# Holding the first store back until most of the fourth load has landed, and fewer, larger DMA packets at the start

## The chip, the cores and the metric

The kernel runs on one core of a Trainium2 chip. The metric is the device time of one execution, in microseconds. Before the change the median of 3 runs is 316.60 us (316.60 to 316.67).

## The reference

Each row of 1024 numbers is divided by the sum of its absolute values:

```python
batch, seq, dim = 32, 512, 1024          # x: float32, 64 MiB
sums = np.sum(np.abs(x), axis=-1, keepdims=True)
return (x / (sums + 1e-8)).astype(np.float32)
```

So 67.11 MB are read from HBM and 67.11 MB written, and every element is read once by a reduction and once by a multiplication in between.

## The kernel before

The input is seen as 16,384 rows of 1024 floats, 128 to each of the 128 partitions. They are cut into 11 tiles. Ten tiles have R = 12 rows per partition (49,152 bytes per partition, 6 MiB in all), the last, tile 10, has 8 (4 MiB). Tiles 0, 1 and 10 together make up a first block of 32 rows per partition that lies together in HBM; every other tile is a block of its own. `piece` gives the part of input or output that belongs to a tile.

There are BUFS = 4 tile buffers. A tile is loaded, normalized in its place and stored from there, so load i+4 can start only when store i has landed.

The order of work is written out by hand under `tc.manual_schedule()`; each engine runs its instructions in program order. Three engines matter:

- SP issues the loads (line 87), which run in DMA queue q1.
- ACT (ScalarE) issues the stores (line 97), which run in q10, and multiplies some rows of some tiles (line 68), one activation per row.
- DVE (VectorE) does the rest of a tile: the sum of absolute values over all its rows (line 47), the added constant (line 54), the reciprocal (line 56), one multiplication of `kv` rows with the reciprocals broadcast (line 58), and `kt` rows one by one (line 65). The table `split` has, for a tile, `kt` and the number `ks` of rows that go to ACT.

Both DMA queues run on the same 16 DMA engines. `max_dma_last_dim` sets how large a piece, in bytes, a DMA cuts the data of a partition into; a piece is a packet. WHOLE (49,152) makes one packet of a partition's 12 rows, HALF (24,576) two. Before the change loads 0 and 1 go in WHOLE packets, all others in HALF; store 0 is two DMAs, its first FIRST = 3 rows in packets of one row (4 * d = 4,096 bytes) and the other 9 in packets of 36,864. Store 8 is two halves, stores 9 and 10 go in WHOLE packets.

The loop over the tiles does compute, store and the load four tiles on. Store 0 is thus issued as soon as tile 0 is normalized, while loads 2 and 3 are still running.

Of the kernel before, what the change touches and what calls it, by code (L numbers as in the profile page):

```python
# [1 line left out]

# [4 lines left out]

FP32 = mybir.dt.float32
EPS = 1e-8


@with_exitstack
def kernel(
    ctx: ExitStack,
    tc: tile.TileContext,
    x: bass.AP,
    out: bass.AP,
):
    nc = tc.nc
    P = nc.NUM_PARTITIONS  # L20

    x_flat = x.flatten_outer_dims()
    out_flat = out.flatten_outer_dims()
    n, d = x_flat.shape

    R = 12
    BUFS = 4
    HEAD = 32
    per_partition = n // P
    assert n % P == 0 and (per_partition - HEAD) % R == 0  # L30
    rows = [R] * ((per_partition - HEAD) // R + 2) + [HEAD - 2 * R]

    def piece(flat, i):
        head = flat[: P * HEAD, :].rearrange("(p r) d -> p r d", p=P)
        if i < 2:
            return head[:, R * i : R * (i + 1), :]
        if i == len(rows) - 1:
            return head[:, 2 * R :, :]
        a = P * (HEAD + R * (i - 2))
        return flat[a : a + P * R, :].rearrange("(p r) d -> p r d", p=P)  # L40

    sbuf = ctx.enter_context(tc.tile_pool(name="sbuf", bufs=BUFS))
    stats = ctx.enter_context(tc.tile_pool(name="stats", bufs=len(rows)))

    def normalize(x_tile, k, kv, kt):
        s = stats.tile([P, R], FP32)
        nc.vector.tensor_reduce(  # L47
            out=s[:, :k],
            in_=x_tile[:, :k, :],
            axis=mybir.AxisListType.X,  # L50
            op=mybir.AluOpType.add,
            apply_absolute_value=True,
        )
        nc.vector.tensor_scalar_add(out=s[:, :k], in0=s[:, :k], scalar1=EPS)  # L54
        inv = stats.tile([P, R], FP32)
        nc.vector.reciprocal(out=inv[:, :k], in_=s[:, :k])  # L56
        if kv:
            nc.vector.tensor_mul(  # L58
                out=x_tile[:, :kv, :],
                in0=x_tile[:, :kv, :],  # L60
                in1=inv[:, :kv].unsqueeze(2).to_broadcast([P, kv, d]),
            )
        for r in range(kv, kv + kt):
            row = x_tile[:, r, :]
            nc.vector.tensor_scalar_mul(out=row, in0=row, scalar1=inv[:, r : r + 1])  # L65
        for r in range(kv + kt, k):
            row = x_tile[:, r, :]
            nc.scalar.activation(  # L68
                out=row,
                in_=row,  # L70
                func=mybir.ActivationFunctionType.Copy,
                scale=inv[:, r : r + 1],
            )

    last = len(rows) - 1
    split = {0: (3, 4), 1: (0, 3), 2: (0, 3), last - 1: (0, 2), last: (4, 4)}

    tiles = {}

    HALF, WHOLE = 24576, 49152
    FIRST = 3

    def load(i):
        x_tile = tiles[i] = sbuf.tile([P, R, d], FP32, name="x_tile")
        nc.sync.dma_start(out=x_tile[:, : rows[i], :], in_=piece(x_flat, i), max_dma_last_dim=WHOLE if i < 2 else HALF)  # L87

    def store(i):
        if i == 0:  # L90
            parts = [(0, FIRST, 4 * d), (FIRST, R, WHOLE)]
        elif i == last - 2:
            parts = [(0, R // 2, HALF), (R // 2, R, HALF)]
        else:
            parts = [(0, rows[i], WHOLE if i >= last - 1 else HALF)]
        for a, b, size in parts:
            nc.scalar.dma_start(
                out=piece(out_flat, i)[:, a:b, :],
                in_=tiles[i][:, a:b, :],
                max_dma_last_dim=size,  # L100
            )

    def compute(i):
        k = rows[i]
        kt, ks = split.get(i, (0, 0))
        normalize(tiles[i], k, k - kt - ks, kt)

    with tc.manual_schedule():
        for i in range(BUFS):
            load(i)  # L110
        for i in range(len(rows)):
            compute(i)
            store(i)
            if i + BUFS < len(rows):
                load(i + BUFS)


# [1 line left out]
_INS = ['x']  # L119
_OUTS = [((32, 512, 1024), 'float32')]  # L120


# [23 lines left out]
```

## Time and profile before

| what | us |
|---|---|
| median of 3 runs | 316.60 |
| the profiled execution | 316.77 |
| its span (first to last instruction) | 315.2 |
| VectorE busy | 260.6 |
| ScalarE busy | 18.5 |
| first load issued, tile 0's reduction starts | 0.73, 17.80 |
| first store issued (its two parts) | 36.78, 38.83 |
| second, third store issued | 61.95, 85.08 |
| load 4 issued | 76.83 |
| last store issued | 293.25 |

Sections of a profile row are read like this. A row of a window shows its bounds in us and its length, then for DVE, ACT and POOL the busy us with the number of instructions in brackets, the granted TensorE clock (TensorE isn't used here), the DMA share and GB/s. The DMA share is the mean busy share of the 16 DMA engines. In windows a packet is counted whole at its start, so that a short window can have a share above 1 or of 0. A row of the DMA queues shows the number of packets, MB and the share of 16 engines' span that they took. A row of waits shows who waited for what: total us, times, longest. In the packet counts, each DMA has besides its data 16 packets of 4 bytes, one from each DMA engine, that tell of its completion.

### The profile page before, as it was taken

The page shows a single profiled execution, that of the slowest core. Times are in us where ns is not written, and L with a number is a line of the kernel's source. Part 1 is how long each engine was busy: PE and PEld are TensorE (multiplying, and loading weights), DVE is VectorE, ACT ScalarE, POOL GpSimd, SP SyncE. Part 2 cuts the span into 40 slices and gives each one's busy share as a digit, 9 for nine tenths or more (in the row PEclk, how much of TensorE's full clock was granted, in tenths as well). Part 3 has the DMA queues.
Part 4 walks back from the last instruction along what each step waited for, and adds up shares of the span by engine and source line. Part 5 has one row for each costly group of instructions (what it writes and reads, how often), then busy time and mean ns, then how long its engine had stood idle before and what let it go on. Part 6 is the DMA issues. An engine that isn't in the chain of part 4 may idle for free.

```text
span 315.2 us, 172 instructions
## 1 busy us (share of the span) xinstructions
DVE 260.6 (83%) x50; ACT 18.5 (6%) x17; POOL 0.2 (0%) x4
## 2 busy tenths in 40 slices
DVE  0079999999999999989996997999699969999000
ACT  0010503004000000000000000000000000203200
POOL 0000000000000000000000000000000000000000
DMA  8999999999999999999999999999999999999997
GB/s 318 480 399 412 437 407 464 411 436 413 415 446 437 415 446 437 415 449 434 415 449 437 412 449 437 412 449 437 415 446 437 415 437 434 432 428 496 399 408 324
DMA packets 5761, 134.22 MB, mean 426 GB/s; under 512 B 385, under 2 KB 385, under 8 KB 769
## 3 DMA queue, kind: packets, MB, share of 16 engines
q1 hardware_dynamic: 2736, 67.11, 49.8%
q10 hardware_dynamic: 3024, 67.11, 49.4%
q14 instruction: 1, 0.00, 0.0%
HBM read 67.11 MB, written 67.11 MB: 426 GB/s over the span
## 4 chain that ended last, share of the span: by engine, by line
DVE 40%; DMA 33%; another core or an unknown queue 18%; ACT 1%; issue 0%; SPq 0%
DVE s L47 23%; DMA x_tile<-in_x_dram 17%; DMA out_dram<-x_tile 16%; DVE x_tile L58 15%; ACT x_tile L68 1%; DVE x_tile L65 1%; DVE inv L56 0%; DVE s L54 0%; SPq L87 0%
## 5 line engine op out<-in xcount | busy, mean ns | idle before, releaser
L47 DVE TENSOR_REDUCE s<-x_tile 128x12 f32<-128x12288 f32 (+1 forms) x11 | 138.2, 12562 | 29.8 <-DMA x_tile<-in_x_dram 29.8
L58 DVE TENSOR_TENSOR x_tile<-x_tile,inv 128x12288 f32<-128x12288 f32 (+3 forms) x10 | 113.6, 11358 | 0.5
L68 ACT ACTIVATE x_tile<-x_tile,inv 128x1024 f32<-128x1024 f32 x16 | 17.2, 1138 | 256.9 <-DVE inv L56 256.9
L65 DVE TENSOR_SCALAR x_tile<-x_tile,inv 128x1024 f32<-128x1024 f32 x7 | 4.8, 749 | 0.0
L56 DVE RECIPROCAL inv<-s 128x12 f32<-128x12 f32 (+1 forms) x11 | 2.5, 226 | 0.4
L68 ACT ACT_TABLE_LOAD x1 | 1.3, 1283 | 17.8 <-DMA x_tile<-in_x_dram 17.8
L54 DVE TENSOR_SCALAR s<-s 128x12 f32<-128x12 f32 (+1 forms) x11 | 1.9, 174 | 0.4
L130 POOL MEMSET const-bfloat16-1.0<- 128x1 bf16 x1 | 0.1, 101 | 0.0
L130 POOL MEMSET const-uint8-127<- 128x1 uint8 x1 | 0.1, 101 | 0.0
L130 POOL MEMSET const-float32-0.0<- 128x1 f32 x1 | 0.1, 98 | 0.2 <-issue 0.2
L130 POOL MEMSET const-float32-1.0<- 128x1 f32 x1 | 0.1, 98 | 0.0
## 6 DMA issues: line engine op xcount, KB each, us to landing
x_tile<-in_x_dram SPq DMA_DIRECT2D x10, 6144.0 KB, 36.9
out_dram<-x_tile ACTq DMA_DIRECT2D x8, 6144.0 KB, 49.1
out_dram<-x_tile ACTq DMA_DIRECT2D x2, 3072.0 KB, 33.4
out_dram<-x_tile ACTq DMA_DIRECT2D x1, 4608.0 KB, 37.9
x_tile<-in_x_dram SPq DMA_DIRECT2D x1, 4096.0 KB, 32.2
out_dram<-x_tile ACTq DMA_DIRECT2D x1, 4096.0 KB, 20.9
out_dram<-x_tile ACTq DMA_DIRECT2D x1, 1536.0 KB, 29.3
```

What stands on the lines that cost most here:

```text
L47: nc.vector.tensor_reduce(out=s[:, :k], in_=x_tile[:, :k, :], axis=mybir.AxisListType.X, op=mybir.AluOpType.add, apply_absolute_value=True,)
L54: nc.vector.tensor_scalar_add(out=s[:, :k], in0=s[:, :k], scalar1=EPS)
L56: nc.vector.reciprocal(out=inv[:, :k], in_=s[:, :k])
L58: nc.vector.tensor_mul(out=x_tile[:, :kv, :], in0=x_tile[:, :kv, :], in1=inv[:, :kv].unsqueeze(2).to_broadcast([P, kv, d]),)
L65: nc.vector.tensor_scalar_mul(out=row, in0=row, scalar1=inv[:, r : r + 1])
L68: nc.scalar.activation(out=row, in_=row, func=mybir.ActivationFunctionType.Copy, scale=inv[:, r : r + 1],)
L130: nc = _bacc.Bacc("TRN2", target_bir_lowering=False, num_devices=1)
```

## The change

The first store waits for a part of the fourth load. Load 3 becomes two DMAs: the first carries 10.5 of the tile's 12 rows of each partition (REST = 10,752 floats, 43,008 bytes), the second the last 1.5 (6,144 bytes). After the work on tiles 0 and 1, ACT gets a small activation that reads one element per partition of tile 3's first row, and so waits for the first of the two DMAs; store 0 stands behind it in ACT's program, and store 1 behind store 0. Tiles 0 and 1 are both computed ahead of it. Store 0 is one DMA in WHOLE packets instead of two DMAs. Loads 2 and 3 go in WHOLE packets too (load 3 in one packet per partition for each of its two parts). In tile 0 one row moves from VectorE's row operations to its broadcast multiplication.

```diff
-    split = {0: (3, 4), 1: (0, 3), 2: (0, 3), last - 1: (0, 2), last: (4, 4)}
+    split = {0: (2, 4), 1: (0, 3), 2: (0, 3), last - 1: (0, 2), last: (4, 4)}
...
-    FIRST = 3
+    REST = R * d - 3 * d // 2
 
     def load(i):
         x_tile = tiles[i] = sbuf.tile([P, R, d], FP32, name="x_tile")
-        nc.sync.dma_start(out=x_tile[:, : rows[i], :], in_=piece(x_flat, i), max_dma_last_dim=WHOLE if i < 2 else HALF)
+        size = WHOLE if i < BUFS else HALF
+        if i < BUFS - 1 or i >= BUFS:
+            nc.sync.dma_start(out=x_tile[:, : rows[i], :], in_=piece(x_flat, i), max_dma_last_dim=size)
+            return
+        flat = x_tile.rearrange("p r d -> p (r d)")
+        source = piece(x_flat, i).rearrange("p r d -> p (r d)")
+        for a, b in ((0, REST), (REST, R * d)):
+            nc.sync.dma_start(out=flat[:, a:b], in_=source[:, a:b], max_dma_last_dim=size)
 
     def store(i):
-        if i == 0:
-            parts = [(0, FIRST, 4 * d), (FIRST, R, WHOLE)]
-        elif i == last - 2:
-            parts = [(0, R // 2, HALF), (R // 2, R, HALF)]
-        else:
-            parts = [(0, rows[i], WHOLE if i >= last - 1 else HALF)]
-        for a, b, size in parts:
+        parts = [(0, R // 2), (R // 2, R)] if i == last - 2 else [(0, rows[i])]
+        for a, b in parts:
             nc.scalar.dma_start(
                 out=piece(out_flat, i)[:, a:b, :],
                 in_=tiles[i][:, a:b, :],
-                max_dma_last_dim=size,
+                max_dma_last_dim=WHOLE if i == 0 or i >= last - 1 else HALF,
             )
...
+    def wait_for_loads():
+        seen = stats.tile([P, 1], FP32, name="seen")
+        nc.scalar.activation(out=seen, in_=tiles[BUFS - 1][:, 0, :1], func=mybir.ActivationFunctionType.Copy)
+
     with tc.manual_schedule():
         for i in range(BUFS):
             load(i)
+        compute(0)
+        compute(1)
+        wait_for_loads()
         for i in range(len(rows)):
-            compute(i)
+            if i > 1:
+                compute(i)
             store(i)
             if i + BUFS < len(rows):
                 load(i + BUFS)
```

## The prediction

> **What bounds the kernel now.** I read the page first, then the stretches (busy time, DMA share and GB/s of a window), then waits and DMA issues.
>
> ```profile
> span 315.2 us, 172 instructions
> DVE 260.6 (83%) x50; ACT 18.5 (6%) x17; POOL 0.2 (0%) x4
> ...
> DMA  8999999999999999999999999999999999999997
> ...
> q1 hardware_dynamic: 2736, 67.11, 49.8%
> q10 hardware_dynamic: 3024, 67.11, 49.4%
> ...
> HBM read 67.11 MB, written 67.11 MB: 426 GB/s over the span
> ```
>
> The DMA engines are busy 99.2% of the span (49.8 + 49.4), q1 (SP) with loads, q10 (ACT) with stores. VectorE is busy 83% only. So the time is bytes over rate, plus start and end; the question is where the rate falls.
>
> ```profile
> 0.00:4.00 4.00, 0.00 (x0) 0.00 (x0) 0.20 (x4) 1.00 0.64 197
> 4.00:36.00 32.00, 18.10 (x4) 5.55 (x5) 0.00 (x0) 1.00 1.00 432
> ...
> 36.00:66.00 30.00, 29.90 (x9) 3.23 (x3) 0.00 (x0) 1.00 1.01 424
> ...
> 66.00:80.00 14.00, 13.90 (x4) 3.23 (x3) 0.00 (x0) 1.00 1.00 434
> 80.00:160.00 80.00, 78.14 (x13) 0.00 (x0) 0.00 (x0) 1.00 1.00 433
> 160.00:240.00 80.00, 71.74 (x13) 0.00 (x0) 0.00 (x0) 1.00 1.00 433
> ```
>
> The last number of a row is GB/s, the one before it the DMA share. Loads alone (4 to 36) run at 432, stores alone (66 to 80) at 434, both together (80 to 240) at 433. Mixing directions therefore costs nothing by itself. One stretch lies lower: 36 to 66, in which the first store's three-row part lies beside the rest of loads 2 and 3. One-microsecond windows show two costs in it:
>
> ```profile
> 13.00:14.00 1.00, 0.00 (x0) 0.00 (x0) 0.00 (x0) 1.00 1.81 786
> ...
> 33.00:34.00 1.00, 1.00 (x1) 1.00 (x2) 0.00 (x0) 1.00 0.91 393
> ...
> 61.00:62.00 1.00, 1.00 (x2) 0.00 (x0) 0.00 (x0) 1.00 1.07 459
> 62.00:63.00 1.00, 1.00 (x1) 0.00 (x0) 0.00 (x0) 1.00 1.51 459
> ```
>
> A packet is counted where it starts. 786 GB/s for 1 us is 16 packets of 49,152 bytes, one per DMA engine, 1.81 us each; 393 is 16 of 24,576, 0.91 us each; 459 is 16 of 24,576 and 16 of 4,096, so a small one takes 1.07 - 0.91 = 0.16 us. From 62 to 63 the same 32 packets took 1.51: 0.44 us lost on all engines. The trace's packet records give the finer figures used below: 159 ns for 4,096 bytes, 912 for 24,576, 1364 for 36,864, 1815 for 49,152, which is about 9 ns a packet plus 36.74 ns per 1000 bytes.
>
> ```profile
> DVE s L47 <- DMA x_tile<-in_x_dram: 29.8, 6, 17.8
> ...
> SPq L87 <- DMA out_dram<-x_tile: 242.1, 8, 63.3
> ```
>
> VectorE waits for loads, and SP's loads wait for stores (a buffer comes free): both hang on the DMA rate. DMA issues (last number: us from issue to landing) of load 0 and store 10:
>
> ```profile
> x_tile<-in_x_dram SPq DMA_DIRECT2D x1, 6144.0 KB, 17.0
> ...
> out_dram<-x_tile ACTq DMA_DIRECT2D x1, 4096.0 KB, 20.9
> ```
>
> **The change, part by part.** The sum is made against the profiled execution: 316.77 us, its span 315.2 and 1.6 around it, 0.17 above the median of 316.60.
>
> *Whole packets in store 0.* Before, each DMA engine carries 24 packets of 4,096 bytes and 8 of 36,864: 24 x 0.159 + 8 x 1.364 = 14.73 us. After, 8 of 49,152: 8 x 1.815 = 14.52. All of it is on the bound: **-0.21**.
>
> *Whole packets in loads 2 and 3.* Load 2: 16 x 0.912 = 14.59 becomes 14.52, **-0.07**. Load 3 becomes 8 packets of 43,008 and 8 of 6,144, by the line above 8 x 1.589 + 8 x 0.235 = 14.59: **0**. The extra load costs SP about 0.4 us of issue (its issues took 0.37 to 0.61 us) before 3 us, while load 0 transfers until 17.8.
>
> *A rule against this part.* Row first: the 4,096-byte pieces took 0.16 us, 25.8 GB/s an engine against 27.1 in a 49,152-byte packet. The Trainium skill (DMA: Bandwidth & Descriptors, Specifications) has line rate from 512 bytes up; read strictly, both packet edits would bring 0 instead of 0.28. I go by the row.
>
> *The slow loads of 36 to 66.* In the packet records the loads' packets between 36.9 and 64.3 took together 0.71 us per DMA engine above their usual 0.912 each: 0.13 until 56, 0.58 from 61 to 64.3 (0.44 of it is the row above). Bounds: all of it goes (-0.71), or none (0). I take **-0.71**: loads and stores of 24,576 bytes lie side by side from 80 to 279 and next to no packet is late there, so it isn't the mixture; small store pieces beside loads are what this stretch alone has, and after the change none are left, nor any load beside the first store's start.
>
> *The new wait.* Loads come first, 14.5 us each. The DMA rows put load 0's landing at 0.73 + 17.0 = 17.7; load 1's at about 32.3 and load 2's would be at 46.8. The 10.5 rows add 8 x 1.589 = 12.7: landing seen at L = 59.5. What is left then? The 1.5 rows are 8 x 0.235 = 1.88 us for each engine. The completion writes of load 0 lie between 16.85 and 17.44 in the records, and waiting engines went on at 17.80, so an engine has been 0.35 to 0.95 us into the rest at L: 0.93 to 1.53 remain, mean 1.24. What has to happen: ACT wakes (0.05, its table load began 17.85 against 17.80), does the 128x1 copy, issues the store (0.04), and the first packets start. The copy is not in the trace: at least 0.10 (the 128x1 memset on POOL), at most 1.13 (ACT's 128x1024 row); nearest is VectorE's 128x12 operation with 0.17, so I take 0.2. Issue to first packet: load 0 was issued at 0.73 on idle DMA engines and its packets start at 1.74 to 2.40, 1.16 later in the mean. Together 0.05 + 0.2 + 0.04 + 1.16 = 1.45, less 1.24: the DMA engines idle **+0.2**. Low end 0 (a copy of 0.1 and earliest start 1.0). High end: store 0 before was issued at 36.78 and its first packet started at 40.54, 3.75 later; then 0.29 + 3.75 - 1.24 = +2.8. I read that delay as queueing, some three load packets of 0.91 (2.7) taken ahead on each engine plus 1.0; load 4, issued at 76.83 behind 24,576-byte stores, started at 80.45, 3.6 later, which fits. Ahead of the new store stand only 0.235 us packets, already counted in the 1.24.
>
> *A second rule.* The row says 1.0 to 1.67 from issue to first packet. The Trainium skill (DMA: Bandwidth & Descriptors, Latency and other measured facts) has about 0.6 us for a DMA issued from SP or ACT; by it the need is 0.89 and the gap 0, which makes the sum 0.2 lower.
>
> *First packets of a stream.* The first 16 packets of load 0 took 0.70 us longer in the mean than 1.815 (hence 197 GB/s in the first 4 us). If the first store's do the same on an idle machine, +0.7; the first store packets before took 159 ns like all others, so I take **0** and keep 0.7 as the end.
>
> *What is queued behind the wait.* On ACT: store 0, store 1 and tile 2's three rows (ready at 75). VectorE does not wait: tile 0 has six broadcast rows (5.49 x 6/5 = 6.6) and two row operations (1.5) instead of 5.49 + 2.0, so it ends 0.5 later, and tile 1 at 62.4. Store 1 is then queued while store 0 transfers until about 75.5, so q10 doesn't run dry. The moved row costs 0: store 0 isn't issued before 59.8 anyway. SP's load 4 waits for store 0, landing at about 75.9 against 38.83 + 37.9 = 76.7 before: no later than now, and while store 1 keeps the engines full.
>
> *The end.* Store 10, issued at 293.25, lands 20.9 later though its 4 MB need 9.7: more than 10 us in the queue. VectorE could be 10 us later and cost nothing; if that cover went, the end would follow VectorE one to one.
>
> Sum: -0.21 - 0.07 - 0.71 + 0.2 = -0.79. 316.77 - 0.79 = 315.98 in the profiled form, **315.8** as median.
>
> **Rivals.**
> 1. *The slow loads stay*, elsewhere: the stall at 62 came once, on all engines, and I have no row that ties it to a store packet. For it: the small packets from 46 to 61 went along without it. Then -0.08: 316.5, no measurable change.
> 2. *The first store starts slowly* like load 0: +0.7, giving 316.5. For it: the 197 GB/s row. Against it: write packets never show lateness here.
> 3. *The other side: the hand-over leaves the DMA engines idle.* Everything depends on 1.24 us of cover. If issue to first packet is 3.75 as for store 0 before, not 1.16, the gap is 2.8 and the time 315.8 + 2.6 = 318.4. It decides (above 317.23) when the gap passes 1.6, which is 2.6 us from issue to first packet. Against it: the queueing reading fits two starts.
> 4. *Nothing changes* because the loads pace everything: excluded for the 0.28 of packets, since the engines are full either way.
>
> **How the numbers follow.** Forecast 0.48, own range 315.4 to 316.3; rival 1 0.22; rival 2 0.14; rival 3 0.12 (a smaller delay gives 317.2 to 318.4); others 0.04. The runs agree within 0.02%, so 0.2% (0.63 us: below 315.97, above 317.23) is about what a measurement can tell from no change. Faster: 0.36 of the forecast, 0.02 of rival 1: 0.38. Slower: 0.12 of rival 3, 0.03 of rival 2 with a wider gap, 0.02 others: 0.17. Same: 0.45. The range reaches from 315.4 (all gains, no gap) to 317.5 (no gains from the slow loads, plus 0.7 and some more gap), leaving out some 0.03 below and 0.13 above.
>
> **What would show it.** In the profile after: no packets below 8 KB but completions and 128 of 6,144; first store issued at about 59.8; windows of 1 us without 1.51 at 459; a window from 61 to 75 at 434; between 60 and 62 at most 0.3 us without packets. Wrong if that hole is 1 us or more, if late packets return around 60, or if load 4 lands after VectorE is done with tile 3 (111.8).

## The result, and the profile after

The change made the kernel slower: 317.63 us median (317.04 to 318.17, 8 runs) against 316.61 (316.46 to 316.68, 8 runs), a ratio of 1.0032 with a 95% interval of 1.002 to 1.0044. The runs of the changed kernel fall into two groups, four from 317.04 to 317.27 and four from 318.00 to 318.17; those of the kernel before lie within 0.22 us. The profiled execution took 317.27 us, 0.50 more than that of the kernel before, with a span of 315.6 against 315.2.

The page of the changed kernel, its head and the DMA queues:

```profile
span 315.6 us, 170 instructions
DVE 260.9 (83%) x49; ACT 18.7 (6%) x18; POOL 0.2 (0%) x4
...
q10 hardware_dynamic: 2624, 67.11, 49.6%
q1 hardware_dynamic: 2624, 67.11, 49.6%
```

5248 data and completion packets instead of 5760: the packets did become fewer. The DMA engines are as busy as before (99.2%), so the time is still theirs. Its stretches, with the bounds that were used for the kernel before (last two numbers: DMA share and GB/s):

```profile
4.00:36.00 32.00, 18.18 (x4) 5.55 (x5) 0.00 (x0) 1.00 1.02 442
36.00:66.00 30.00, 29.90 (x8) 3.43 (x4) 0.00 (x0) 1.00 0.97 419
66.00:80.00 14.00, 13.90 (x4) 3.23 (x3) 0.00 (x0) 1.00 1.07 441
80.00:160.00 80.00, 77.70 (x13) 0.00 (x0) 0.00 (x0) 1.00 1.00 427
160.00:240.00 80.00, 71.80 (x10) 0.00 (x0) 0.00 (x0) 1.00 1.01 433
```

With packets of 49,152 bytes the GB/s of a window depend on how many packets happen to start in it, so GB/s is to be divided by the share: bytes for each microsecond that the engines call themselves busy. 4 to 36 gives 433 and 36 to 66 gives 432, where the kernel before had 420 (424 at a share of 1.01). The slow stretch from 36 to 66 is gone. But 66 to 80 gives 412, where it had 434, and 80 to 160 gives 427 at a full share. One-microsecond windows find the place:

```profile
78.00:79.00 1.00, 1.00 (x1) 0.78 (x1) 0.00 (x0) 1.00 1.12 467
79.00:80.00 1.00, 1.00 (x1) 0.00 (x0) 0.00 (x0) 1.00 1.58 442
80.00:81.00 1.00, 1.00 (x1) 0.00 (x0) 0.00 (x0) 1.00 0.55 123
81.00:82.00 1.00, 1.00 (x1) 0.00 (x0) 0.00 (x0) 1.00 0.88 369
82.00:83.00 1.00, 1.00 (x1) 0.00 (x0) 0.00 (x0) 1.00 0.97 418
```

442 GB/s in one microsecond are 18 packets of 24,576 bytes; at 0.912 us each they would make a share of 1.03, and the row shows 1.58. In the packet records, a store packet on each of the 16 DMA engines that started between 79.66 and 80.20 took 1.46 to 1.81 us, up to twice its time. All engines lose 0.8 us there, and then the first packets of load 4 start, at 81.29. In the same place the kernel before lost nothing:

```profile
79.00:80.00 1.00, 1.00 (x1) 0.00 (x0) 0.00 (x0) 1.00 0.97 418
80.00:81.00 1.00, 1.00 (x1) 0.00 (x0) 0.00 (x0) 1.00 0.97 418
81.00:82.00 1.00, 1.00 (x1) 0.00 (x0) 0.00 (x0) 1.00 0.91 393
```

There load 4 began at 80.45 beside the same store 1, in the same packets. The waits of VectorE hardly moved, 30.2 us for loads in all (29.8 before).

**The ledger.** I call *late time* the sum, over packets, of what they took beyond their usual duration (9 ns and 36.74 ns per 1000 bytes), divided by 16 engines. From 6 us on it is 0.71 us before and 1.20 after. The usual durations of all packets sum to 0.27 us less. The completions of the last store come at 313.28 to 313.83 before and at 313.52 to 314.32 after: the engines end 0.35 later in the mean, and they end 0.24 us further apart, which makes the last one 0.49 later. So -0.27 from packets, +0.44 late time (with the start, where it fell by 0.05), +0.18 that the records don't assign (short gaps between packets), +0.14 from the spread of the ends: +0.49, and the span grew by 0.47. This is the ledger of an execution of the faster group; what makes the other four about 0.9 us longer is not in it.

### The profile page after: what moved, and what is told of

It reads as the page before. It is cut to its first block, busy times and chain, and to the rows that moved or that the text cites. A ratio compares the mean times of both kernels' runs of the same rounds, so it can differ in the third digit from the quotient of the medians.

```text
span 315.6 us, 170 instructions
## 1 busy us (share of the span) xinstructions
DVE 260.9 (83%) x49; ACT 18.7 (6%) x18; POOL 0.2 (0%) x4
## 2 busy tenths in 40 slices
DMA packets 5248, 134.22 MB, mean 425 GB/s; under 512 B 384, under 2 KB 384, under 8 KB 512
## 4 chain that ended last, share of the span: by engine, by line
DVE 38%; DMA 33%; another core or an unknown queue 18%; issue 3%; ACT 1%; SPq 0%; DVEq 0%
DVE s L47 23%; DMA x_tile<-in_x_dram 17%; DMA out_dram<-x_tile 15%; DVE x_tile L58 13%; DVE x_tile L65 1%; ACT x_tile L68 1%; DVE inv L56 0%; DVE s L54 0%; SPq L89 0%; DVEq L151 0%; DVEq L58 0%
## 5 line engine op out<-in xcount | busy, mean ns | idle before, releaser
L47 DVE TENSOR_REDUCE s<-x_tile 128x12 f32<-128x12288 f32 (+1 forms) x11 | 138.2, 12562 | 30.2 <-DMA x_tile<-in_x_dram 30.2
```

What stands on the lines that cost most here:

```text
L47: nc.vector.tensor_reduce(out=s[:, :k], in_=x_tile[:, :k, :], axis=mybir.AxisListType.X, op=mybir.AluOpType.add, apply_absolute_value=True,)
```

## The experiments

Each kernel is an edit of the kernel before or of the changed kernel. Late times are those of the one profiled execution of each kernel, whose time and span stand in the table; it can lie away from the median, by 1.1 us with whole packets at 80 and by 0.8 with half tiles. Letters in the expectations name theories: A, the wait brings the stall; B, an accident; C, one stall in every execution, at the first meeting of large stores and loads; D, large first store packets bring the loss; E, I, the held store makes the meeting at 80 stall, whatever went before; F, G, the stall grows with the packets, or is a fixed latency; H, a pause of some 20 us without loads makes it; L, the first longer spell of loads beside stores costs it, and later ones are free.

| kernel | median, us | before in the same runs | profiled (its span) | late time 6 to 36 | 36 to 66 | 66 to 84 | 84 to 140 |
|---|---|---|---|---|---|---|---|
| before (profile) | | | 316.77 (315.2) | 0.00 | 0.69 | 0.01 | 0.00 |
| changed | 317.63 | 316.61 | 317.27 (315.6) | 0.01 | 0.07 | 0.94 | 0.18 |
| the same again | 317.32 | 316.56 | 318.02 (316.4) | 0.02 | 0.34 | 1.03 | 0.18 |
| packets only | 317.38 | 316.56 | 317.38 (315.4) | 0.00 | 1.29 | 0.00 | 0.00 |
| wait only | 317.59 | 316.56 | 317.61 (315.8) | 0.01 | 0.18 | 0.98 | 0.13 |
| wait for 12 rows | 318.65 | 316.56 | 318.63 (316.7) | 0.00 | 0.09 | 0.97 | 0.13 |
| FIRST = 4 | 316.76 | 316.60 | 316.74 (315.1) | 0.09 | 0.43 | 0.07 | 0.13 |
| early scratch store | 319.96 | 316.60 | 319.91 (318.1) | 0.63 | 0.08 | 0.97 | 0.13 |
| whole packets at 80 | 319.26 | 316.60 | 320.40 (318.8) | 0.00 | 0.04 | 1.57 | 0.87 |
| quarter packets at 80 | 317.87 | 316.60 | 317.40 (315.8) | 0.01 | 0.13 | 1.01 | 0.16 |
| load 4 late | 316.63 | 316.59 | 316.80 (315.2) | 0.00 | 0.61 | 0.01 | 0.01 |
| half tiles | 319.04 | 316.59 | 319.87 (317.9) | 0.01 | 0.20 | 1.41 | 0.39 |
| small loads in the pause | 318.14 | 316.59 | 317.79 (316.1) | 0.00 | 0.03 | 0.88 | 0.22 |
| 3 rows early, 4,096 bytes | 316.78 | 316.57 | 316.58 (315.0) | 0.01 | 0.62 | 0.02 | 0.01 |
| 1 row early, 4,096 bytes | 316.71 | 316.57 | 316.62 (315.0) | 0.01 | 0.02 | 0.69 | 0.11 |
| 3 rows early, 12,288 bytes | 317.16 | 316.57 | 317.28 (315.7) | 0.00 | 0.56 | 0.84 | 0.12 |
| loads 2 and 3 whole | 316.69 | 316.57 | 316.63 (315.0) | 0.01 | 0.68 | 0.01 | 0.00 |
| wait for 4 rows | 316.86 | 316.52 | 316.93 (315.3) | 0.01 | 1.09 | 0.00 | 0.00 |

### The changed kernel again

> The changed kernel again, unaltered, on another occasion. Its 8 runs fell into two groups, 317.0 to 317.3 and 318.0 to 318.2, and its trace shows one stall of all DMA engines of about 0.8 us at 79.7 to 82, when load 4's first packets come. Theory A (a stall that the wait brings, at the return from stores alone to loads beside stores): the stall is there again near 80, the time stays 0.5 to 1.5 us above the kernel before, and if the profiled run is of the slower group a second stall of some 0.9 us shows in it. Theory B (an accident of that one execution): no stall near 80, and a time of 315.8 to 316.3.

317.32 us (317.24 to 318.02), ratio 1.0028 (1.0016 to 1.004). The stall is there again, late time 1.00 from 77 to 84. B falls. The profiled execution was the longest of the six (318.02); it has no second stall of 0.9, which A expected. Between its span and that of the profiled execution above lie 0.78 us: 0.35 are late time, most of it in the loads before the first store (0.27 from 36 to 66), and 0.42 come because its last engine ends 0.89 us behind the mean of the 16, not 0.47. Why the engines end further apart in some executions stays open.

### Each half of the change alone

The kernel before with whole packets and no wait:

```diff
-max_dma_last_dim=WHOLE if i < 2 else HALF)
+max_dma_last_dim=WHOLE if i < BUFS else HALF)
...
-            parts = [(0, FIRST, 4 * d), (FIRST, R, WHOLE)]
+            parts = [(0, R, WHOLE)]
```

> The kernel before with whole packets alone: store 0 as one DMA of 49,152-byte packets, loads 2 and 3 in whole packets; no wait, load 3 in one DMA, the old split of tile 0. Theory A (the loss comes from the wait): 316.6 - 0.28 = 316.3 if the stall at 62 us stays somewhere, 315.6 to 315.8 if that stall came from 4,096-byte pieces. Theory C (a stall of 0.6 to 0.9 us comes once in every execution, the first time that large store packets lie beside loads): a stall at about 40 us, when store 0's first packets start beside load 2, and 316.3. Theory D (large first store packets bring the loss): 317 or more.

317.38, ratio 1.0025 (1.0015 to 1.0034): slower without any wait. Windows of this kernel, at the start of store 0 and at load 4's old place:

```profile
40.00:44.00 4.00, 4.00 (x1) 0.00 (x0) 0.00 (x0) 1.00 1.15 369
78.00:84.00 6.00, 6.00 (x1) 0.33 (x1) 0.00 (x0) 1.00 1.02 438
```

369 over 1.15 is 321 GB/s: the stall, 1.29 us of late time, is where store 0's whole packets first meet loads. From 78 to 84 nothing is late. The 317 of D and the stall at 40 of C both came, but the stall is larger than C's 0.6 to 0.9. Only part of the time is the stall's, though: the span grew by 0.27 us (0.59 more late time, 0.36 less in the usual durations of the packets), while the time outside the span was 1.9 to 2.0 us in all nine runs, where the kernel before has 1.6 to 1.7. What that part is, the profile doesn't show; four more kernels of the table have 1.7 to 2.0 there.

The wait alone, with the packets and the row split of before (in the changed kernel, store 0 again in two DMAs, loads 2 and 3 in half packets):

```diff
-        size = WHOLE if i < BUFS else HALF
+        size = WHOLE if i < 2 else HALF
...
-        parts = [(0, R // 2), (R // 2, R)] if i == last - 2 else [(0, rows[i])]
+        if i == 0:
+            parts = [(0, FIRST, 4 * d), (FIRST, R, WHOLE)]
...
```

> The changed kernel with the packets and the row split of the kernel before: the wait, with load 3 in two DMAs, is what is left of the change. Store 0 is two DMAs again, 3 rows in 4,096-byte packets and 9 rows; loads 2 and 3 in half packets. Theory A (the wait brings the stall): a stall near 80 us as in the changed kernel, and 317.3 + 0.28 = 317.6 to 318.5. Theory D (whole packets bring it): 316 to 316.5. Theory C: a stall too, near 80.

317.59 (1.0032; 1.0021 to 1.0044), 0.93 us late from 77 to 84: A and C as expected, and D falls as the only cause. Either half of the change alone brings a stall of its own, in different places. Together they make one.

### The price of the hand-over

```diff
-        if i < BUFS - 1 or i >= BUFS:
+        if True:
```

> The changed kernel with load 3 as one DMA, so that the first store waits for all 12 rows and no 1.5 rows are left to transfer beside the hand-over. This measures the cover. By the prediction's sum the DMA engines then idle 1.45 us and the skew of the completions, 1.5 to 2.0 us at 59 to 63, against next to none in the changed kernel, and the time is 1.3 to 1.9 us above it. A rival: the hand-over costs nothing since the end is bound elsewhere, and the time equals the changed kernel's.

318.65, 1.33 us above the changed kernel in the same runs (317.32). The windows of this kernel:

```profile
60.00:61.00 1.00, 1.00 (x1) 0.00 (x0) 0.00 (x0) 1.00 0.01 0
61.00:62.00 1.00, 1.00 (x1) 0.20 (x1) 0.00 (x0) 1.00 0.00 0
62.00:63.00 1.00, 1.00 (x2) 0.00 (x0) 0.00 (x0) 1.00 1.89 786
```

Its last load packets end at 60.66 in the mean and the first store packets start at 62.22: 1.56 us of idle engines, inside the expected 1.5 to 2.0. (The ends are those of the completion writes.) In the changed kernel the two lie 0.02 us apart. The 1.5 rows do what the prediction's sum said, and the loss isn't there.

### Where large stores first meet loads

FIRST = 4 in the kernel before, so that the small packets outlast load 3:

```diff
-    FIRST = 3
+    FIRST = 4
```

> The kernel before with FIRST = 4 instead of 3: store 0's part in 4,096-byte packets has four rows, so that it outlasts load 3 and the large packets of store 0's second part never lie beside loads; large stores first meet loads near 80 us, as in the changed kernel. In every trace so far one stall of all DMA engines comes where large store packets first lie beside loads: 62 us before (0.5 us), 40 us with whole packets alone (1.2), 79 to 82 us with the wait (0.85 to 0.95). Theory C (one such stall in every execution, at the first meeting of large stores and loads): no stall at 62, one of 0.8 to 0.9 us near 80, and 316.6 - 0.5 + 0.85 + 0.07 = 317.0. Theory E (the meeting at 80 is harmless in a kernel without the wait, as it is in the kernel before, and only the wait makes it stall): no stall at all and 316.6 - 0.5 + 0.07 = 316.2.

316.76, ratio 1.0006 (0.9997 to 1.0015): no measurable change. The stall at 62 is gone, and from 78 to 84, where large stores now first meet loads, next to nothing is late (0.07 us). So C, as worded, falls. But E's 316.2 didn't come either:

```profile
38.00:42.00 4.00, 4.00 (x3) 0.00 (x0) 0.00 (x0) 1.00 1.01 397
78.00:84.00 6.00, 6.00 (x1) 0.46 (x1) 0.00 (x0) 1.00 0.92 393
```

397 GB/s lie at a share of 1.01 where 0.92 would do: the late loads moved to the start of the small stores, 0.35 us of late time in these four. All late time of this kernel is 0.72 us, as in the kernel before (0.71).

A short early store, in the changed kernel:

```diff
+    scratch = nc.dram_tensor("scratch", (32, 6, d), FP32, kind="Internal").ap()
+    def early_store():
+        nc.scalar.dma_start(out=scratch, in_=tiles[0][:32, :6, :], max_dma_last_dim=HALF)
...
+        early_store()
         compute(0)
```

> The changed kernel with one more store, of 32 packets of 24,576 bytes (two for each DMA engine) from the first 6 rows of tile 0 as loaded, into a scratch tensor in HBM, issued when load 0 has landed at 17.7 us, beside load 1. Its bytes cost 0.79 MB / 433 GB/s = 1.8 us. Theory C (one stall in an execution, at the first meeting): a stall of 0.9 to 1.8 us near 20 us and none near 80; the time is 317.3 + 1.8 + 0 to 0.9. Theory E (it is this meeting, after 20 us of stores alone): the stall near 80 stays as it is, 0.85 us, and 317.3 + 1.8 = 319.1 with no stall near 20, or about 320 with one more.

319.96. Two stalls: 0.63 us near 20, and 0.97 near 82. Two store packets on each engine meet their stall and don't save the later one. C falls for good; E, with one more stall, fits.

### Packet size and pause

Load 4 and store 1 in whole packets, and in quarters (in the changed kernel; the edit is that for whole packets):

```diff
-        size = WHOLE if i < BUFS else HALF
+        size = WHOLE if i <= BUFS else HALF
...
-max_dma_last_dim=WHOLE if i == 0 or i >= last - 1 else HALF,
+max_dma_last_dim=WHOLE if i <= 1 or i >= last - 1 else HALF,
```

> The changed kernel with load 4 and store 1, which meet near 80 us, in packets of 49,152 instead of 24,576 bytes. Theory F (the stall is about one packet of the size that meets, as each engine lets the other queue go ahead once): 1.6 to 1.8 us instead of 0.85, and the time 317.3 + 0.85 - 0.15 (fewer packets) = 318.0. Theory G (the stall is a fixed latency): 0.85 and 317.2.

> The changed kernel with load 4 and store 1 in packets of 12,288 bytes. Theory F (the stall is about one packet of the size that meets): 0.45 us instead of 0.85, the time 317.3 - 0.4 + 0.29 (32 more packets of about 9 ns on each engine) = 317.2; the stall may then come back when packets of 24,576 bytes first meet, near 100 us. Theory G (a fixed latency): 0.85 and 317.6.

With 49,152 bytes:

```profile
78.00:84.00 6.00, 6.00 (x1) 1.02 (x1) 0.00 (x0) 1.00 1.01 328
```

With 12,288:

```profile
78.00:84.00 6.00, 6.00 (x1) 0.93 (x1) 0.00 (x0) 1.00 1.02 371
```

With 49,152 bytes the late time near 80 is 1.55 us, F's size, half of it in store packets ahead of load 4 and half in load 4's own first packets; another 0.87 comes later, most of it from 96 to 106. The time is 319.26 us, far above F's 318.0. The profiled execution, 320.40, is the longest of the four (the others took 319.10 to 319.32), and its last engine ends 2.35 us behind the mean of the 16. With 12,288 the late time is 0.98, not 0.45: a store packet takes up to 0.447 longer, twice its time, but two in a row do. So near 80 F holds upwards and G downwards: smaller packets than 24,576 gain nothing.

The kernel before with load 4 held back behind tile 2's work:

```diff
+            if i == 2:
+                tick = stats.tile([P, 1], FP32, name="tick")
+                nc.vector.tensor_scalar_add(out=tick, in0=tiles[0][:, 0, :1], scalar1=EPS)
+                load(BUFS)
+                load(BUFS + 1)
+                load(BUFS + 2)
+            elif i > 2 and i + BUFS < len(rows):
```

> The kernel before with load 4 held back: a small VectorE operation behind tile 2's work reads tile 0's buffer, so load 4 is issued at about 85 us and not at 76.8. Loads are then absent from 65.5 to about 88 us, 23 us and not 15; stores 1 and 2 keep the DMA engines full meanwhile, and VectorE waits some us for tile 4, which the queued stores cover. Theory H (the stall near 80 of the held kernels comes because no load has moved for some 20 us; the kernel before stays under that with 15 us): a stall of 0.7 to 0.9 us of all DMA engines at about 88, beside the one at 62, and 317.3 to 317.5. Theory I (it depends on the wait or the store's packets, not on the length of the pause): no stall at 88 and 316.6.

316.63, ratio 1.0003 (0.9993 to 1.0012). Load 4 was issued later than meant, at 91.26, and no load packet moved from 65.2 to 95.0. The return cost nothing:

```profile
92.00:98.00 6.00, 5.97 (x2) 0.00 (x0) 0.00 (x0) 1.00 1.04 451
120.00:126.00 6.00, 1.40 (x1) 0.00 (x0) 0.00 (x0) 1.00 1.03 442
150.00:160.00 10.00, 10.00 (x2) 0.00 (x0) 0.00 (x0) 1.00 1.00 433
```

All three give 429 to 434 GB/s per share. The last window holds the reverse: stores pause from 144.6 to 154.8, as VectorE is late by then, and start again beside loads without a late packet. In this kernel a pause of 30 us is harmless, so H falls.

Shorter pauses in the changed kernel: buffers of 6 rows for tiles 0, 4 and 8, and three small loads in the pause.

```diff
+        if i % BUFS == 0:
+            tiles[i] = []
+            for a in (0, H):
+                part = half.tile([P, H, d], FP32, name="x_tile")
+                tiles[i].append(part)
+                nc.sync.dma_start(out=part, in_=piece(x_flat, i)[:, a : a + H, :], max_dma_last_dim=HALF)
+            return
...
```

> The changed kernel with the buffer of tiles 0, 4 and 8 cut into two of 6 rows, each with its own load, work and store in 24,576-byte packets. Half of load 4 can go when half of store 0 has landed, so the loads pause from 61 to about 72 us, 11 us instead of 20. Theory H (a pause of some 20 us makes the stall): no stall at 72, none near 80, and 317.3 - 0.9 + 0.15 (load 0 and store 0 in twice as many packets) = 316.5. Theory I: a stall of about 0.85 us where load 4's first packets come, now near 72, and 317.3 or more.

```diff
+    def keep_reading():
+        for j in range(3):
+            spare = spare_pool.tile([16, d], FP32, name="spare")
+            for _ in range(2):
+                nc.scalar.activation(out=spare, in_=tiles[1][:16, 0, :], func=mybir.ActivationFunctionType.Copy)
+            nc.sync.dma_start(out=spare, in_=x_flat[j * 16 : j * 16 + 16, :])
...
+            if i == 1:
+                keep_reading()
...
```

> The changed kernel with three small loads into spare buffers during the pause: 16 packets of 4,096 bytes each (one for each DMA engine, 0.16 us), issued at about 65, 67.5 and 69.5 us, each released by two activations on the otherwise idle ACT. Loads are then absent for 10 us at most. Theory H: the stall near 80 goes, and 317.3 - 0.85 + 0.5 (the bytes) = 316.9. Theory I: the stall stays, and 317.3 + 0.5 = 317.8.

Half tiles: 319.04 (318.26 to 319.87, the last being the profiled execution), with a stall at 72 to 74, where the first half of load 4 comes, and a second from 78 to 82, where the second store ends and the third is just being issued. Small loads: 318.14, with 0.76 us near 80. H falls here too; I's 317.8 is the nearer.

### An earlier spell of stores beside loads

The changed kernel, with some rows of store 0 sent as soon as tile 0 is done, and the rest held:

```diff
+    EARLY = 3
+    def early_store():
+        nc.scalar.dma_start(out=piece(out_flat, 0)[:, :EARLY, :], in_=tiles[0][:, :EARLY, :], max_dma_last_dim=4 * d)
...
+        early_store()
         compute(1)
```

> The changed kernel, of whose store 0 three rows go out as soon as tile 0 is done, in 4,096-byte packets beside loads 2 and 3; the other nine wait as in the changed kernel. Theory L (the first time that loads and stores run side by side for a longer while costs a settling stall, large with large store packets, small with small ones, and later meetings are free): the stall near 80 shrinks to 0.1 at most, some 0.1 to 0.4 us of late loads come from 40 to 60, and the time is 317.3 - 0.85 + 0.2 + 0.3 = about 316.9, 316.4 at best. Theory I (the held store makes the meeting at 80 stall, whatever went before): the stall of 0.85 stays, and 317.5 to 317.8.

> The same with one row early, 8 packets of 4,096 bytes on each DMA engine, so that loads and stores run side by side for some 15 us only. Theory L: a meeting of this length still settles and the stall near 80 is gone or halved, 316.5 to 316.9; the scratch store of two packets, 2 us long, didn't settle anything. Theory I: the stall stays, 317.3 to 317.5.

> The same with three rows early in packets of 12,288 bytes. Theory L: a settling stall of 0.4 to 0.9 us near 40, as store packets are larger, and next to none at 80; about 317. Theory I: the stall at 80 stays, with a second near 40: 317.6 to 318.

Three small rows: 316.78, ratio 1.0007 (0.9998 to 1.0017), and the stall at 80 is gone, as L expected. The windows of this kernel:

```profile
58.00:61.00 3.00, 3.00 (x1) 0.00 (x0) 0.00 (x0) 1.00 0.74 259
78.00:84.00 6.00, 6.00 (x1) 0.88 (x1) 0.00 (x0) 1.00 0.94 406
```

406 at 0.94 is the pace of the kernel before, 432. The price came earlier: 259 at 0.74 is 350, in the last large packets of load 3, while small stores still run beside them. With 0.62 us from 36 to 66 it is larger than L's 0.1 to 0.4.

The windows with one small row:

```profile
40.00:48.00 8.00, 8.00 (x1) 0.00 (x0) 0.00 (x0) 1.00 0.96 414
78.00:84.00 6.00, 6.00 (x1) 0.80 (x1) 0.00 (x0) 1.00 0.98 373
```

And with three rows in 12,288 bytes:

```profile
40.00:48.00 8.00, 8.00 (x1) 0.00 (x0) 0.00 (x0) 1.00 0.95 379
78.00:84.00 6.00, 6.00 (x1) 0.82 (x1) 0.00 (x0) 1.00 1.01 377
```

One small row: 316.71, the time that L gave, but the stall near 80 stays at 0.68, so L's condition isn't just some spell of 15 us. Three rows in 12,288 bytes: 317.16 (1.0019; 1.0009 to 1.0028), with 0.56 from 40 to 48 and 0.83 near 80: both, as I expected and not L. In these two the early part had landed at 55 and 58, before the held part was issued at 60.7 and 63.8; with three small rows stores were still under way when the rest of store 0 was issued behind them.

Loads 2 and 3 of the kernel before in whole packets, and nothing else:

```diff
-max_dma_last_dim=WHOLE if i < 2 else HALF)
+max_dma_last_dim=WHOLE if i < BUFS else HALF)
```

> The kernel before with loads 2 and 3 in whole packets and nothing else changed. By the packet count it saves 16 packets of 9 ns on each DMA engine, 0.14 us: 316.45. If the size of the load packets that a stall meets matters, the stall at 62 grows from 0.5 to about 1 us, and the time is 316.9 to 317.1.

316.69 (1.0006; 0.9996 to 1.0015), the stall at 60 as large as before (0.55 us). The late packets of the packets-only kernel thus come from store 0's whole packets, not from the loads'.

### The wait moved

In the changed kernel the first store waits for 4 rows of load 3:

```diff
-    REST = R * d - 3 * d // 2
+    REST = 4 * d
```

> The changed kernel, where the first store waits for 4 of load 3's 12 rows instead of 10.5 (4 and 8 rows are its two DMAs). The store is issued at about 51.6 us and its whole packets run beside some 8 rows of load 3. Theory L (the first longer meeting of loads and large stores costs the stall, later ones are free): a stall of 0.9 to 1.3 us near 53, none near 80 or where load 4 comes, and 317.2 to 317.6, as in the changed kernel. Theory I (a held first store makes load 4's meeting stall, whatever went before): a stall where load 4 comes, with or without one near 53: 317.3 to 318.5.

316.86, ratio 1.001 (1.000 to 1.002), 0.3 below what either theory gave. The windows:

```profile
52.00:58.00 6.00, 5.93 (x3) 3.32 (x4) 0.00 (x0) 1.00 1.05 377
78.00:84.00 6.00, 6.00 (x1) 0.73 (x1) 0.00 (x0) 1.00 1.01 434
```

For comparison the changed kernel:

```profile
78.00:84.00 6.00, 6.00 (x1) 0.78 (x1) 0.00 (x0) 1.00 1.00 369
```

The stall, 1.09 us, follows the store to 53 to 57, and 78 to 84 is clean at 430. I falls: a held first store doesn't make load 4 stall, once large stores have run beside load 3. L's place and size came out.

### What is left standing

In every kernel the DMA engines lose at least 0.6 us, where loads and stores first come together, at the end of that first spell, or at the next meeting. With small store packets ahead it is 0.6 to 0.7 in all (before, FIRST = 4, load 4 late, three small rows early, loads whole), 0.85 with one small row early, with large ones 1.1 to 1.3 in most. It is 1.5 to 1.9 with the early scratch store, with three rows of 12,288 bytes and in the second profile of the changed kernel, and more with half tiles and with whole packets at 80. Later meetings cost at most 0.2 if stores went on without a break from that first spell until the loads had ended; an early spell that had run dry before (two packets, one row, three rows of 12,288 bytes) did not make the meeting at 80 free. That is a description made after the runs, not a mechanism, and the later stalls of half tiles and of whole packets at 80 lie outside it. What in the DMA engines settles, and why a break of 10 us in the stores at 145 us costs nothing while one of 8 us at 55 does, I could not tell apart.

One thing the records show about the place: with large packets much of the loss comes before the two streams run side by side. With whole packets alone the late load packets start at 40.47 to 40.87, and store 0's first packet at 43.39; with the wait for 4 rows the late loads start from 53.48 on, most of their late time at 54 to 56, and the first store packet at 56.63; in the changed kernel the late store packets start up to 80.20, and load 4's first packet at 81.29. So in these three the running stream slows mainly while the other one has been issued and has not yet moved a packet.

No version beat the kernel before beyond its measurement.

## Why the prediction was wrong

- *Packets, -0.21 and -0.07.* Right: the usual durations of all packets sum to 0.27 us less.
- *The new wait, +0.2.* Right in mechanism, a little too dear. Tile 3's first part was seen at 59.50 (the sum had 59.5), the copy took 0.20, the first store packets started at 60.52, 1.01 after the issue. The issue began at 59.51, beside the copy and not behind it, which took the gap from 0.2 to 0.02. Without the 1.5 rows it is 1.56 us. The page of the Trainium skill that I weighed (DMA: Bandwidth & Descriptors, Latency and other measured facts) has 0.6 us to the first byte; measured are 1.01 here and 0.88 with the wait for 12 rows (issued at 61.28, first packet at 62.16), nearer to the row of before.
- *First packets of a stream, 0.* Right (load 0's first packets were 0.73 longer, not 0.70): the held store's first packets took at most 0.05 longer, 0.07 us of late time in all. Rival 2 fell, and rival 3 with it.
- *What is queued behind the wait, and the end.* Right: load 4 was issued at 76.03, VectorE was not held (tile 0 ended 0.3 later, where the terms add up to 0.6 and the text has 0.5), the last store was issued at 293.98 and still queued.
- *The slow loads of 36 to 66, -0.71.* This is the step that failed. The stretch did get clean (late time 0.07 from 36 to 66), but 1.13 us came from 66 to 140, 0.91 of it from 77 to 84, most of that in store packets just ahead of load 4. The inference was: from 80 to 279 loads and stores lie side by side and no packet is late, so the mixture isn't the cause, small pieces are. The runs say the opposite. Small pieces are not the cause: with whole packets in their place the late time is 1.29 instead of 0.68 (packets only against loads 2 and 3 whole). Nor are small pieces all that the stretch has alone, for store 0's 36,864-byte packets begin in it too, at 64.96, right behind the late loads. And that the meetings after 80 are clean doesn't show that they are free: with the first meeting beside loads 2 and 3 taken out, the one with load 4 stalls (wait only, the changed kernel twice); with stores running beside load 3 until it ends it doesn't (wait for 4 rows, three small rows early). Removing the first meeting moved the loss to the next and made it larger. Why a meeting costs this, and why an earlier one can spare the next, stays open.
- *Rival 1* had the right idea, that the stall stays elsewhere, and the wrong price. It took 0.71 as the most that could come back, since that was the bound of what could be removed. 1.20 came, and the engines ended further apart. The range ended at 317.5 for the same reason: no term for a stall that grows. The median of 317.63 lies above it because half of the eight executions took 318.00 or more; on the second occasion the median was 317.32. That the time then fell inside the range is no merit of the sum, which had the sign of this term wrong.

The Trainium skill (DMA: Bandwidth & Descriptors, Queues, rings and completion order) says that a DMA engine takes turns between the queues that have work, a packet at a time. The settled stages agree: from 88 to 140 us, with packets of 24,576 bytes on both sides, the kernel before moved 11.26 MB of loads and 11.23 MB of stores. The section gives no cost for a queue that joins. The runs show a loss of 0.6 us or more around such places, and none of them shows that taking turns is its cause.

## What to carry to other kernels

A stretch that runs clean late in a profile does not show that the same mixture is free the first time; look at the first place where it occurs, and price what is removed there as something that may come back, larger. In the records, look also at the stream that was already running, ahead of the first packet of the one that joins. In a kernel bound by DMA throughput, a store held behind loads costs little at the hand-over if a small last load covers the latency (0.02 us of idling with 1.5 rows of cover, 1.56 without). Starting stores early, in small packets beside the loads, cost less here than holding them back.

## What the runs showed of the hardware that was not expected

- All 16 DMA engines together slowed to about half pace for some 1.8 us when loads joined a stream of stores near 80 us, in most of the kernels with a held first store: store packets of 24,576 bytes took up to 1.81 us instead of 0.91, of 12,288 bytes 0.91 instead of 0.46, two in a row. With whole packets alone, load packets of 49,152 bytes just ahead of the first store's took up to 3.3 us instead of 1.8.
- The size of the pieces of a first store mattered far beyond the 9 ns a packet: replacing 4,096-byte pieces by whole packets saved 0.2 us of packet time and cost 0.6 us of late packets (1.29 against 0.68 with the same loads).
- In the kernel before, with load 4 late, neither a pause of 30 us in the loads nor one of 10 us in the stores brought the stall back later in the execution.
